# A hybrid attention layer on one core: transposes moved from TensorE to VectorE and DRAM, copies of sample rows in DRAM, state sums on VectorE

## The chip, the core and the metric

The kernel runs on one core of a Trainium2 chip. The metric is the device time of one execution in microseconds (us). A core has five engines that run their own instruction streams: PE (TensorE, matmuls and transposes), ACT (ScalarE), DVE (VectorE), POOL (GpSimd) and SP, which only issues DMAs here. POOL and ACT can issue DMAs too. Data lies in DRAM, in SBUF (128 partitions) and, for matmul outputs, in PSUM.

## What is computed

One inference step of a decoder layer with two mixers, for a prompt of 512 new tokens and for 8 running sequences with one new token each (the *samples*). Model width is 1024; all is float32. Cut to what the change touches:

```python
h = x @ w_in                                   # 1024 -> 3600 columns
qa, ka, va, za, ga, qb, kb, vb, gb = split(h)
# mixer A: gated linear attention, 4 heads, dk 64, dv 128, chunks of 64 tokens
S_t = diag(a_t) S_{t-1} + k_t^T v_t ;  o_t = q_t S_t     # samples: one step from state_gla
o_a = o_a * rsqrt(mean(o_a^2) + eps) * gla_norm_g
# mixer B: 8 heads of 64; keys at distances 0,d,2d,..,window for
# (window, d) = (128,1), (512,4), (2048,16), with a relative-position bias
o_b = merge of three softmaxes by their denominators    # samples: 1024 cached keys + the new one
mix = concat(o_a * silu(ga), o_b * silu(gb))
y   = mix @ w_out
x_new = layer_norm(sqrt(2) * x + y) * ln_g + ln_b
```

Outputs are x_new of prompt and samples, the final states of both, and the key and value rows to keep.

## The kernel before

Each product of a float32 matrix is made as three reduced-precision matmuls (high x high, high x low, low x high), so weights and activations are split into pairs named hi_ and lo_, mh and ml. The columns of w_in are worked off in pieces (qa, qb, kb, and so on); mixer B's prompt attention and mixer A's chunks run between them; and the output projection with w_out comes last: for tokens 0-255 (tiles y0, y1) the projection is first made with the tokens in the free dimension (ps_yf) and turned, for tokens 256-511 (y2, y3) with the tokens in the partitions (ps_y). The layer norm of a token tile runs on DVE and ACT as its last piece arrives. The sample rows travel as 8 further columns beside the prompt's.

**What sets the order.** The functions are generators that yield one operation at a time; a planner takes them as tasks and issues, engine by engine, the operation that its table TIMES has due first. TIMES holds one line per task, a start and the steps to each following operation, so it fixes the order on every engine. `At(mark)` holds a task until another one has set a mark; `Need(tag, ...)` holds it until a buffer of a kind is free (kinds: "g" for gate-sized tiles, "sv" for cached values, "r" for raw weights, and others). Every operation is recorded in the helper `issue`, so the profile gives line 672 for all of them, and groups are told apart by their tile names. QUEUE says which engine issues three kinds of turning DMAs: outputs y on POOL, values v on SP, keys k on POOL.

**Turning through DRAM.** `store_blocks` (line 1036) writes a tile, in which DVE has transposed each 32x32 block by itself, to a scratch array in DRAM, and `load_turned` (line 1040) reads the blocks back in exchanged places, which completes the transpose. Keys, values and the outputs of tokens 0-255 take this way: yw (blocks transposed) goes to ysc by a store, then yx comes from ysc by a load, both on POOL's queue, and DVE adds yx to y.

**mix_a(u, j)** (line 1926) finishes mixer A for 128 tokens: u is the half of the prompt, j the tile in it. oa holds o_a with tokens in partitions. Four PE transposes put it into a PSUM bank (ps_oat); three DVE operations multiply it by the norm's weight gn and the gate ga, and `split` makes the pair mha, mla for the output projection.

**The samples in mixer B.** `sample_queries` (line 1697) writes the 8 queries to DRAM (qsd) and reads each one back to all 128 partitions (qbc); POOL multiplies the cached keys (past) by it, DVE sums to logits. `sample_softmax` writes the probabilities to DRAM (psd_s), `sample_values` (line 1773) reads them back to the partitions of each cached-value tile (pb, 16 loads for 8 samples), and POOL multiplies (vv).

**sample_state** (line 1838) makes the samples' new states, four sequences at a time: s is the old state, v the new values read to all partitions. ACT multiplies s by the decay a_s (8 pieces of 128x128), SP writes it to the output; ACT multiplies v by the key ka_s (8 pieces), and POOL adds it to the output in DRAM by an accumulating DMA:

```python
for x, scale in ((s4, a_s), (v4, ka_s)):
    for bb in range(4):
        for m in range(2):
            yield S.mul(x[:, bb, m, :], x[:, bb, m, :], scale[:, m, i * 4 + bb:i * 4 + bb + 1])
    x = x.rearrange("p b m v -> p (b m) v")
    yield D.dma_start(to, x) if scale is a_s else G.dma_start(to, x, accum_op=ALU.add)
```

`last_norm` and `early_mean` close tile y3: early_mean takes the mean and variance of three quarters of the row ahead of time (tiles tail, mv), last_norm adds the last quarter behind the last matmul.

## Time and profile before

| | us |
|---|---|
| runs | 273.28, 274.27, 274.56 (median 274.27) |
| the profiled execution: time | 273.52 |
| the profiled execution: span | 271.7 |
| DMA traffic | 57.82 MB, mean 213 GB/s |
| last matmul ends (start 263.66, 0.28 long) | 263.94 |

The span is counted from the first to the last instruction in the trace; the execution's own time is 1.8 us longer. The page's second part cuts the span into 40 slices and gives each engine's busy share in tenths:

```profile
PE   8999999999999999999999999999999999999980
DVE  3844979999999877397999789687787586226994
POOL 3000000000183954550073451441916021611200
DMA  7995798244999798958999964979589995798132
```

A row of a timeline reads: start, duration, engine, line, operation, output tile <- input tiles with their shape, a count if neighbours are run together, and in brackets the idle time of the engine ahead of it and what ended it. The rows of a group read: busy time in all and mean ns of one, then idle time ahead of them and its releasers. Rows of stretches give, behind the bounds, the length and then the busy time of PE, PEld (weight loads), DVE, ACT and POOL, the granted clock, the DMA engines' share, and GB/s.

### The profile page before, as it was taken

How to read it: one execution, taken by the hardware profiler on the slowest of the kernel's cores; microseconds unless marked ns; L12 is line 12 of the kernel's file. 1: busy time of each engine (PE TensorE's matmuls, PEld its weight loads, DVE VectorE, ACT ScalarE, POOL GpSimd, SP SyncE). 2: the span in 40 equal slices, each digit the busy share in tenths (PEclk: the TensorE clock that was granted, in tenths of full speed). 3: DMA queues.
4: the chain of work that ended last, by engine and by line, in shares of the span. 5: the costliest groups of instructions: out<-in, count | busy, mean ns of one | idle time of the engine just before them, and what ended most of it. 6: DMA issues, size and time to landing. Idle time of an engine off the chain costs nothing. (4 is left out here: it accounts for less than half of the span.)

```text
span 271.7 us, 7366 instructions
## 1 busy us (share of the span) xinstructions
PE 262.8 (97%) x2851; PEld 247.2 (91%) x2851; DVE 209.3 (77%) x525; ACT 155.2 (57%) x462; POOL 77.4 (28%) x94
## 2 busy tenths in 40 slices
PE   8999999999999999999999999999999999999980
PEld 5999999999999999989989999989999999988880
DVE  3844979999999877397999789687787586226994
ACT  4735765565557763345956566536779855612720
POOL 3000000000183954550073451441916021611200
PEclk9999999999999999999999999999999999999995
DMA  7995798244999798958999964979589995798132
GB/s 207 354 251 127 188 280 212 74 120 131 280 309 202 221 317 157 303 148 253 271 232 328 292 177 143 270 176 281 167 214 245 286 230 89 159 322 179 77 154 82
DMA packets 70551, 57.82 MB, mean 213 GB/s; under 512 B 18157, under 2 KB 62355, under 8 KB 70517
## 3 DMA queue, kind: packets, MB, share of 16 engines
q1 hardware_dynamic: 67237, 53.36, 71.4%
q0 software_dynamic: 2848, 3.67, 7.1%
q8 instruction: 22, 0.36, 0.6%
q10 hardware_dynamic: 432, 0.33, 0.4%
q14 instruction: 12, 0.10, 0.1%
HBM read 48.31 MB, written 9.83 MB: 214 GB/s over the span
## 5 line engine op out<-in xcount | busy, mean ns | idle before, releaser
L672 POOL TENSOR_TENSOR past<-past,qbc 128x256 f32<-128x256 f32 x32 | 26.9, 871 | 82.5 <-DMA qbc<-qsd 81.0
L672 POOL TENSOR_TENSOR vv<-vv,pb 128x256 f32<-128x256 f32 x32 | 28.8, 930 | 43.6 <-DMA pb<-psd_s 40.8
L672 ACT ACTIVATE pr<-pr,ms 128x128 f32<-128x128 f32 (+3 forms) x48 | 22.8, 490 | 8.5 <-DVE ms L672 8.4
L672 ACT COPY pt<-ps_pt 128x256 f32<-128x256 f32 (+1 forms) x25 | 8.2, 347 | 9.5 <-PE ps_pt L672 9.4
L672 ACT ACTIVATE d<-d 128x512 f32<-128x512 f32 x11 | 6.9, 644 | 10.6 <-DVE d L672 10.6
L672 PE MATMUL ps_ka<-xx,hi_ka 128*128 128x264 f32 (+1 forms) x64 | 12.8, 295 | 0.0
L672 DVE CUSTOM_DVE_ANT_0 pr<-ps_s,strip 128x128 f32<-128x128 f32 (+3 forms) x32 | 11.7, 405 | 0.9 <-PE ps_s L672 0.9
L672 DVE TENSOR_REDUCE lt<-past 128x8 f32<-128x512 f32 x16 | 10.5, 671 | 0.7 <-POOL past L672 0.7
L672 PEld LDWEIGHTS ps_ka<-xx,hi_ka 128*128 128x128 f32 x64 | 10.3, 200 | 0.6 <-ACT hi_ka L672 0.6
L672 PE MATMUL ps_pt<-cf,pr 128*128 128x128 f32 x56 | 10.6, 276 | 0.3 <-DVE va L672 0.3
L672 DVE TENSOR_REDUCE o_pv<-vv 128x4 f32<-128x1024 f32 x8 | 9.7, 1208 | 0.0
L672 DVE SCALAR_TENSOR_TENSOR y<-y,yx 128x256 f32<-128x256 f32 x6 | 2.4, 420 | 8.8 <-DMA yx<-ysc 8.8
L672 PE MATMUL ps_ka<-xx,lo_ka 128*128 128x264 f32 (+1 forms) x32 | 9.0, 291 | 0.0
L672 DVE STREAM_TRANSPOSE yw<-feat_y 128x256 f32<-128x256 f32 x6 | 3.9, 642 | 5.6 <-ACT feat_y L672 5.6
L672 ACT CAST mhb<-gb 128x256 fp32r<-128x256 f32 x8 | 3.2, 406 | 8.2 <-DVE gb L672 7.6
L672 DVE TENSOR_SCALAR pr<-pr,ms 128x320 f32<-128x320 f32 (+3 forms) x16 | 7.7, 489 | 0.2
L672 PEld LDWEIGHTS ps_pt<-cf,pr 128*128 128x128 f32 x56 | 6.7, 140 | 1.0 <-DVE va L672 0.5
L672 ACT ACTIVATE qh<-ps_qb 128x128 fp32r<-128x128 f32 x16 | 5.2, 433 | 3.5 <-PE ps_qb L672 3.4
L672 ACT COPY feat_y<-ps_yf 128x256 f32<-128x256 f32 x8 | 3.0, 372 | 7.3 <-PE ps_yf L672 7.1
L672 DVE TENSOR_TENSOR gb<-gb,obT 128x256 f32<-128x256 f32 x8 | 6.1, 767 | 1.3 <-ACT gb L672 1.3
L672 PE MATMUL ps_pv<-pt,v 128*64 128x128 f32 (+1 forms) x80 | 6.9, 318 | 0.0
L672 DVE SCALAR_TENSOR_TENSOR ql<-ps_qb,qh 128x128 fp32r<-128x128 f32 x16 | 5.6, 397 | 1.6 <-ACT qk L672 1.5
(567 smaller groups left out, 1072.3 us busy)
## 6 DMA issues: line engine op xcount, KB each, us to landing
past<-in_ck_dram SPq DMA_DIRECT2D x8, 512.0 KB
vv<-in_cv_dram SPq DMA_DIRECT2D x8, 512.0 KB
pb<-psd_s SPq DMA_DIRECT2D x16, 256.0 KB
s<-in_state_dram SPq DMA_DIRECT2D x4, 512.0 KB
qbc<-qsd SPq DMA_DIRECT2D x8, 256.0 KB
y<-in_xp_dram SPq DMA_DIRECT2D x4, 512.0 KB
x_raw<-in_xT_dram SPq DMA_DIRECT2D x6, 260.0 KB
out_dram<-y SPq DMA_DIRECT2D x3, 512.0 KB
```

What stands on the lines that cost most here:

```text
L672: getattr(eng.eng, op.fn)(*op.args, **op.kw)
```

## The change

Three parts, and a new TIMES table.

1. **mix_a for tokens 0-255** no longer transposes on PE. DVE transposes the 32x32 blocks of oa into a "g" buffer ow, SP stores it to a new scratch array osc and reads it back turned, and the three multiplications read ow in place of PSUM. Tokens 256-511 keep their PE transposes.
2. **Sixteen copies.** qsd and psd_s hold each row 16 times, and a read takes each copy for 8 partitions. The order of heads and samples changes so that one read of pb covers the whole tile: 8 loads of 512 KB with rows of 4 KB in place of 16 loads of 256 KB with rows of 1 KB. Constants and the bias table follow the new order.
3. **sample_state** adds on DVE: ACT multiplies s as before, DVE computes s <- v * ka_s + s in 8 pieces, and one SP DMA writes the sum. ACT's pieces on v and the accumulating DMA go.

```diff
+COPIES = 16
-QUEUE = dict(y="G", v="D", k="G")
+QUEUE = dict(y="G", v="D", k="G", o="D")
...
-    qsd = dram.tile([NB, 512], F32, name="qsd")
-    psd_s = dram.tile([64, 256], F32, name="psd_s")
+    qsd = dram.tile([COPIES, 4 * NB + 4, P], F32, name="qsd")
+    psd_s = dram.tile([COPIES, 32 + 4, 256], F32, name="psd_s")
+    def reads(x, first, n, width):
+        return bass.AP(tensor=x.tensor, offset=x.offset + first, ap=[[x.shape[1] * x.shape[2], COPIES], [0, n // COPIES], [1, width]])
+    osc = {(u, j): scratch(f"osc{u}{j}", HA) for u in (0,) for j in range(2)}
...
     def sample_queries():
-        yield D.dma_start(by_tile(qsd), q_rows)
+        yield D.dma_start(qsd[:, :4 * NB].rearrange("r q d -> q r d"), q_rows[:, None, :].to_broadcast([32, COPIES, P]))
...
-            yield D.dma_start(qbc, qsd[bi:bi + 1, :].to_broadcast([P, 512]))
+            yield D.dma_start(qbc, reads(qsd, bi * 512, P, 512))
...
-        yield D.dma_start(psd_s, p_s[:, :256])
+        for v in range(2):
+            yield D.dma_start(psd_s[v * COPIES // 2:(v + 1) * COPIES // 2, :32].rearrange("r q k -> q r k"),
+                              p_s[v * 32:v * 32 + 32, None, :256].to_broadcast([32, COPIES // 2, 256]))
...
             pb = yield Need("sv", f"pb{bi}", [P, 4, 256])
-            row = psd_s[bi * 8:bi * 8 + 8, :]
-            for h2 in range(2):
-                yield D.dma_start(pb[h2 * 64:h2 * 64 + 64],
-                                  bass.AP(tensor=row.tensor, offset=row.offset + h2 * 256, ap=[[0, 64], [512, 4], [1, 256]]))
+            yield D.dma_start(pb.rearrange("p m k -> p (m k)"), reads(psd_s, bi * 1024, P, 1024))
...
     def sample_state():
-            for x, scale in ((s4, a_s), (v4, ka_s)):
-                for bb in range(4):
-                    for m in range(2):
-                        yield S.mul(x[:, bb, m, :], x[:, bb, m, :], scale[:, m, i * 4 + bb:i * 4 + bb + 1])
-                x = x.rearrange("p b m v -> p (b m) v")
-                yield D.dma_start(to, x) if scale is a_s else G.dma_start(to, x, accum_op=ALU.add)
-            free(v4, s4)
+            each = [(bb, m, i * 4 + bb) for bb in range(4) for m in range(2)]
+            for bb, m, n in each:
+                yield S.mul(s4[:, bb, m, :], s4[:, bb, m, :], a_s[:, m, n:n + 1])
+            for bb, m, n in each:
+                yield V.scalar_tensor_tensor(s4[:, bb, m, :], v4[:, bb, m, :], ka_s[:, m, n:n + 1], s4[:, bb, m, :], op0=ALU.mult, op1=ALU.add)
+            free(v4)
+            yield D.dma_start(to, s4.rearrange("p b m v -> p (b m) v"))
+            free(s4)
...
     def mix_a(u, j):
         yield At(f"oa_done{2 * u + j}")
+        oa = B[f"oa{u}"]
+        by_dram = not u
+        if by_dram:
+            ow = yield Need("g", f"ow{u}{j}", [P, HA, P])
+            yield blocks(ow, oa[:, j, :])
+            free(oa)
+            yield store_blocks(queue["o"], osc[u, j], ow)
+            yield load_turned(queue["o"], ow.rearrange("p h (a j) -> p (h a) j", j=32), osc[u, j])
         yield At(f"mla{u}")
         yield At(f"ga{u}_done", 4)
...
-        ps = yield bank("t", "ps_oat")
-        for hd in range(HA):
-            yield T.transpose(ps[:, hd * P:hd * P + P], oa[:, j, hd * P:hd * P + P], ident)
+        if not by_dram:
+            ps = yield bank("t", "ps_oat")
+            for hd in range(HA):
+                yield T.transpose(ps[:, hd * P:hd * P + P], oa[:, j, hd * P:hd * P + P], ident)
+            free(oa)
+            ow = ps.rearrange("p (h t) -> p h t", t=P)
```

New lines of TIMES for the tasks of the first part (before: 215978 and 216564, eight steps each):

```
mix_a|0|0 193600 1000 4400 17600 1358 489 884 1142
mix_a|0|1 198799 1 5835 12465 962 388 1446 585
```

**On SP, around the w_out loads.** The rows of SP's queue around the last four w_out loads, before (raw_wo are the pieces of w_out, v<-vad the samples' values, s the samples' states, y<-in_xp the residual rows; in brackets what a row waits for):

```order
L672 DMA v_3435<-vad 64x8x128 [waits DVE_49]
L672 DMA raw_wo__3444<-in_w_out_dram 128x2x512 [waits DMAHW6_49,Activation_49]
L672 DMA v_3435<-vad 64x8x128 [waits DMAHW7_49]
L672 DMA raw_wo__3477<-in_w_out_dram 128x2x512 [waits DMAHW0_49,DMAHW1_49,DVE_49,Activation_49]
L672 DMA raw_wo__3548<-in_w_out_dram 128x2x512 [waits DMAHW2_49,DVE_49,Activation_49]
L672 DMA out_dram<-s_3264 128x8x128 [waits Activation_49]
L672 DMA raw_wo__3595<-in_w_out_dram 128x2x512 [waits DMAHW6_49,DMAHW3_49,DVE_49]
L672 DMA y_3642<-in_xp_dram 128x1024 [waits DMAHW4_49,PE_49]
```

and now:

```order
L677 DMA osc_103<-ow_3296 128x4x128 [waits DMAHW6_49,DVE_49]
L677 DMA v_3333<-vad 64x8x128 [waits DVE_49]
L677 DMA v_3333<-vad 64x8x128 [waits DMAHW0_49]
L677 DMA ow_3296<-osc_103 128x16x32 [waits DMAHW6_49,DMAHW1_49,PE_49]
L677 DMA osc_104<-ow_3442 128x4x128 [waits DMAHW2_49,DVE_49]
L677 DMA raw_wo__3460<-in_w_out_dram 128x2x512 [waits DMAHW3_49,Activation_49]
L677 DMA raw_wo__3492<-in_w_out_dram 128x2x512 [waits DMAHW4_49,DVE_49,Activation_49]
L677 DMA ow_3442<-osc_104 128x16x32 [waits DMAHW5_49,DMAHW2_49,PE_49]
L677 DMA raw_wo__3558<-in_w_out_dram 128x2x512 [waits DVE_49,Activation_49]
L677 DMA raw_wo__3597<-in_w_out_dram 128x2x512 [waits DMAHW7_49,DMAHW3_49,DVE_49]
L677 DMA y_3644<-in_xp_dram 128x1024 [waits DMAHW0_49,PE_49]
```

The two stores and two loads of ow stand among the last four w_out loads, and the write of the first states (out_dram<-s) has left this place; it stands behind the loads of w_s and avg now, and that of the second states behind y, gamma and beta.

**On DVE, ahead of mixer A's gate.** Where lo_wo__3605, the products of the third last w_out piece, is made, the rows before:

```order
L672 TENSOR_TENSOR lo_wo__3605<-raw_wo__3477,hi_wo__3604 128x512
L672 SCALAR_TENSOR_TENSOR ga_3237<-ps_oat,gn,ga_3237 128x2x128 x2
L672 SCALAR_TENSOR_TENSOR ga_3237<-ps_oat,gn,ga_3237 128x2x64 x4
```

and now (lo_wo__3607 is the same piece):

```order
L677 SCALAR_TENSOR_TENSOR s_3275<-v_3333,ka_s,s_3275 128x128 x2
L677 TENSOR_TENSOR lo_wo__3607<-raw_wo__3492,hi_wo__3606 128x512
L677 SCALAR_TENSOR_TENSOR s_3275<-v_3333,ka_s,s_3275 128x128 x3
L677 SCALAR_TENSOR_TENSOR ga_3241<-ow_3296,gn,ga_3241 128x2x128
L677 SCALAR_TENSOR_TENSOR ga_3241<-ow_3442,gn,ga_3241 128x2x128
L677 SCALAR_TENSOR_TENSOR ga_3241<-ow_3296,gn,ga_3241 128x2x64
L677 SCALAR_TENSOR_TENSOR ga_3241<-ow_3442,gn,ga_3241 128x2x64
```

The first eight state sums stand directly ahead of the multiplications by the gate, and these read ow.

**On POOL, the end of its queue.** Before (ysc and yx are store and load of the turned outputs):

```order
L672 DMA out_dram<-v_3435 128x8x128
L672 DMA ysc_95<-yw_3803 128x4x128
L672 DMA ysc_96<-yw_3837 128x4x128
L672 DMA yx_3891<-ysc_95 128x16x32
L672 DMA yx_3928<-ysc_96 128x16x32
L672 DMA ysc_97<-yw_3875 128x4x128
L672 DMA out_dram<-v_3729 128x8x128
L672 DMA yx_4016<-ysc_97 128x16x32
```

and now:

```order
L677 DMA ysc_96<-yw_3797 128x4x128
L677 DMA ysc_97<-yw_3831 128x4x128
L677 DMA yx_3884<-ysc_96 128x16x32
L677 DMA ysc_98<-yw_3869 128x4x128
L677 DMA yx_3916<-ysc_97 128x16x32
L677 DMA yx_3983<-ysc_98 128x16x32
```

Both accumulating DMAs are gone, and the third store stands ahead of the second load.

More of the change, by code (lines that the diff above doesn't have):

```diff
@@ L109, in __init__ @@
             run = 4 * min(run_of(x) for x in aps)
-            rate = 130 if run <= 128 else 175 if x.ap[0][1] <= 64 else 340 if run >= 4096 else 230
-            self.xfer = max(4 * total(x) / rate, 200)
+            rows = x.ap[0][1] * (x.ap[1][1] if x.ap[1][0] == 0 else 1)
+            y = aps[aps[0].tensor.space != bass.MemoryType.DRAM]
+            copies = math.prod(c for step, c in y.ap[1:] if step == 0)
+            rate = 130 if run <= 128 else 175 if rows <= 64 else 340 if run >= 4096 else 230
+            copied = total(x) // copies
+            self.xfer = max(4 * copied / rate, 200)
             self.late = 600 * (rate == 175)
@@ L247 @@
+evac|ps_ka00|0 23728 1
 evac|ps_ka10|0 24419 175
@@ L297 @@
+evac_f|ps_vb0_f1|1 83824a 2706 -191 588 8171
+sample_logit|3|past3|qbc3 89592 154 1 1177 2468 1220
+evac|ps_vb0_2|2 90137a
 scores|0|1 89774 946
-evac|ps_vb0_2|2 90137a
+sample_logit|4|past4|qbc4 96447 700 1354 1 2215 995
+softmax|1|2|ps_s12|pr12 91602 1396 981 150a 26274 273 1407 108 581a
 softmax|0|2|ps_s02|pr02 91359 1327 1444 871a 23920 823 1 1 1a
-softmax|1|2|ps_s12|pr12 91602 714 1663 150a 26274 273 1407 218 471a
+softmax|0|3|ps_s03|pr03 92687 554 949 804a 23928 827 242 109 299a
+softmax|1|3|ps_s13|pr13 92692 548 2460 1352 23352 1 1569 218 145
@@ L376 @@
-softmax|7|3|ps_s73|pr73 167352 2344 1267 122a 8 2024 1707 1 5
-evac_f|ps_va1_f1|1 169131 66 1808 78 6
+scores|3|1 164789 1
+softmax|6|2|ps_s62|pr62 165736 1619 1519 345 831 521 2064 798 217a
+softmax|6|3|ps_s63|pr63 166837 1902 793 190 1063 299 2131 109 557a
+softmax|7|2|ps_s72|pr72 165733 1100 525 249a 2540 249 38 138 306a
+softmax|7|3|ps_s73|pr73 167352 2344 699 690a 8 2024 1707 1 371a
+sample_value|5|vv5|pb5 184673 7 2 1 5285
+evac_f|ps_va1_f0|0 165732 1 411 3 5a
+evac_f|ps_va1_f1|1 167605a 1a 3399 78 425a
@@ L744, in trunk @@
     ssq, rmss = cst("ssq", [P, TT * HA]), cst("rmss", [P, TT * HA])
-    q_s, k_s = cst("q_s", [P, 4, NB]), cst("k_s", [P, 4, NB])
+    q_w, k_w = cst("q_s", [P, NB, 4]), cst("k_s", [P, NB, 4])
+    q_s, k_s = (x.rearrange("p b m -> p m b") for x in (q_w, k_w))
     q_rows = cst("q_rows", [32, P])
@@ L964, in fills @@
         raw = B["rb_raw"]
-        yield S.copy(rb[:64], raw)
-        yield V.tensor_tensor(rb[32:64], raw[32:], rb[32:64].bitcast(F32), op=ALU.subtract)
+        to, by_v = rb.rearrange("p v b m -> p b v m"), raw.rearrange("p b (m v) -> p b v m", v=2)
+        yield S.copy(to[:64], by_v)
+        yield V.tensor_tensor(to[32:64], by_v[32:], rb.bitcast(F32).rearrange("p v b m -> p b v m")[32:64], op=ALU.subtract)
+        yield S.copy(rbt.rearrange("p (v m) -> p v m", v=2), rb[:, :, 0])
         free(raw)
@@ L1062, in sample_rows @@
         ps = yield bank("t", "ps_rows")
-        yield T.transpose(ps[:32, :P], x.rearrange("p m b -> p (m b)"), ident)
+        yield T.transpose(ps[:32, :P], x, ident)
         yield copy(rows, ps[:32, :P])
@@ L1233, in bias_table @@
             pt = yield bank("t", "ps_tab")
-            yield T.matmul(pt[:HB, :c.stop - c.start], rb[:, 0, :], ct[:, c], start=True, stop=True)
+            yield T.matmul(pt[:HB, :c.stop - c.start], rbt, ct[:, c], start=True, stop=True)
             yield copy(tsb[:, to], pt[:HB, :c.stop - c.start])
@@ L1512, in sample_v @@
             yield V.memset(rows, 0.0)
-        yield from sample_rows(x, rows[:32])
+        yield from sample_rows(x.rearrange("p m b -> p (m b)"), rows[:32])
         yield D.dma_start(out, rows[:32])
@@ L1698, in sample_queries @@
         yield At("qb", 8)
-        yield from sample_rows(q_s, q_rows)
-        yield D.dma_start(by_tile(qsd), q_rows)
+        yield from sample_rows(q_w.rearrange("p b m -> p (b m)"), q_rows)
+        yield D.dma_start(qsd[:, :4 * NB].rearrange("r q d -> q r d"), q_rows[:, None, :].to_broadcast([32, COPIES, P]))
         for bi in range(NB):
@@ L1714, in sample_logit @@
         for k in range(2):
-            yield V.tensor_reduce(lt[:, k, bi * 8:bi * 8 + 8], past[:, k].rearrange("p (h d) -> p h d", d=64), axis=AX.X, op=ALU.add)
+            yield V.tensor_reduce(lt[:, k].rearrange("p (v b m) -> p b m v", v=2, b=NB)[:, bi],
+                                  past[:, k].rearrange("p (m v d) -> p m v d", v=2, d=64), axis=AX.X, op=ALU.add)
         free(past)
@@ L1725, in sample_softmax @@
         k_rows = yield Need("t1", "k_rows", [32, P])
-        yield from sample_rows(k_s, k_rows)
-        yield D.dma_start(by_tile(kw_s), k_rows)
+        yield from sample_rows(k_w.rearrange("p b m -> p (b m)"), k_rows)
+        yield D.dma_start(kw_s.rearrange("b (m d) -> (b m) d", d=P), k_rows)
         prod = yield Need("t1", "prod", [32, P])
```

233 lines of the change are left out of this document (111 added, 122 removed).

## The prediction

> **What bounds the kernel now.** I read the page's busy table first, then the table of stretches, then the waits of PE, then the chain that ended last.
>
> ```profile
> PE 262.8 (97%) x2851; PEld 247.2 (91%) x2851; DVE 209.3 (77%) x525; ACT 155.2 (57%) x462; POOL 77.4 (28%) x94
> ...
> 4.00:264.00 260.00, 259.61 (x2845) 245.97 (x2843) 204.02 (x504) 152.64 (x458) 75.09 (x86) 1.00 0.82 218
> 264.00:271.70 7.70, 0.00 (x0) 0.00 (x0) 4.17 (x13) 0.83 (x3) 0.00 (x0) 0.64 0.21 72
> ...
> PE warm_ps L672 <- PEq L2354: 0.8, 1, 0.8
> PE ps_pt L672 <- DVE va L672: 0.3, 1, 0.3
> ```
>
> From 4 to 264 us PE is busy 259.61 of 260 us at a granted clock of 1.00, and it waits 1.1 us in the whole program. Up to 264 us, only fewer or shorter matmuls, or a new wait of PE, can move the time. Waits of POOL and ACT up to there cost nothing now. Behind PE's last matmul lie 7.7 us in which VectorE closes the last rows. The chain of waits says what came last there:
>
> ```profile
> 253.94 3.00 DVE y L672 x3
> ...
> 267.95 0.40 DVE y L672
> ```
>
> From 253.94 us to the end the chain lies on VectorE alone, ten us before PE is done. So the end has two near bounds, PE's last matmul and VectorE's own queue, and I need to know by how much VectorE is late:
>
> ```profile
> 260.80 0.28 PE L672 MATMUL ps_y<-hi_wo__3484,mla 128*128 128x258 f32 x1
> 263.66 0.28 PE L672 MATMUL ps_y<-hi_wo__3484,mla 128*128 128x256 f32 x1
> ...
> 250.48 0.76 DVE L672 SCALAR_TENSOR_TENSOR y<-y,yx 128x256 f32<-128x256 f32 x2 [2.13 <-DMA yx<-ysc]
> ...
> 262.28 0.41 DVE L672 SCALAR_TENSOR_TENSOR y<-y,ps_y 128x256 f32<-128x256 f32 x1
> 266.80 1.54 DVE L672 SCALAR_TENSOR_TENSOR y<-y,tail,beta 128x256 f32<-128x256 f32 x3
> ...
> 263.97 0.47 ACT L672 ACTIVATE sq_y<-ps_y,tail 128x256 f32<-128x256 f32 x1 [4.60 <-PE ps_y L672]
> ```
>
> The second-last output group (128x258) ends at 261.08 us, and VectorE reads it at 262.28: it is 1.2 us late. Its last idle time is the 2.13 us before 250.48, in which it waits for the load of yx; after that its queue is full until 266. If that load came early enough, the close would hang on PE alone: ACT's square starts 0.03 us behind the last matmul either way, and VectorE's last three writes could stand up to 1.2 us nearer to it.
>
> **The change part by part.**
>
> *Transposes of tokens 0-255.* Eight PE transposes go (two tiles of four); those of tokens 256-511 stay.
>
> ```profile
> 215.31 1.04 PE L672 MATMUL ps_oat<-cf,oa 128*128 128x128 f32 x8
> 216.10 0.37 PE L672 MATMUL ps_yf<-mhb,hi_wo__3268 128*128 128x264 f32 x1
> ```
>
> The eight start at 215.31 and the next matmul at 216.10, so PE gains 0.79 us. All that follows on PE moves up by this, if nothing new holds it. In their place stand two VectorE stream transposes of 128x512, two stores and two loads of 256 KB on SP's queue. The multiplications by the gate stay and read SBUF in place of PSUM; I cost that swap at nothing, since it changes an operand only (the same instruction on PSUM: 1.90 us for six).
>
> ```profile
> L672 DVE STREAM_TRANSPOSE kx<-kd 128x512 f32<-128x512 f32 x2 | 2.1, 1100 | 0.0
> ...
> 216.38 1.90 DVE L672 SCALAR_TENSOR_TENSOR ga<-ps_oat,gn,ga 128x256 f32<-128x256 f32 x6
> 218.98 1.28 DVE L672 TENSOR_TENSOR mla<-ga,mha 128x512 fp32r<-128x512 f32 x2
> ...
> 224.35 0.28 PE L672 MATMUL ps_yf<-mha,hi_wo__3438 128*128 128x264 f32 x1
> ...
> 205.00:216.00 11.00, 11.00 (x95) 11.00 (x94) 6.30 (x15) 9.42 (x37) 3.71 (x5) 1.00 0.93 242
> ...
> 200.44 0.15 DVE L672 TENSOR_TENSOR lo_wo__3329<-wsum,hi_wo__3328 128x4 fp32r<-128x4 f32 x1
> ```
>
> Two transposes of 1.10 us cost VectorE 2.2 us. They hide: it is busy 6.30 of 11 us in 205-216. The round trip is the risk. The new order puts the second transpose directly ahead of the row that ran at 200.44, so it would end near 201.6, and its store can go about 203, behind a load of v. PE needs mla at 224.35 now, 223.56 with the gain; behind the load stand half of the six multiplications (0.95) and both halves of mla (1.28), 2.2 us. So store and load together may take 223.6 - 2.2 - 203 = **18.4 us** before PE waits. The nearest rows are the outputs' own round trip, of the same 256 KB and the same 32x32 blocks:
>
> ```profile
> L672 POOL DMA_DIRECT2D yx<-ysc x3: 1153/1163/1171, 232.5 to 245.5; - x3
> ...
> DMA to landing us min/median/max: 5.0/8.6/9.4
> ...
> L672 POOL DMA_DIRECT2D ysc<-yw x3: 756/767/798, 228.8 to 236.2; - x3
> ...
> DMA to landing us min/median/max: 2.8/2.8/8.6
> ```
>
> Shortest 2.8 + 5.0 = 7.8 us, median 11.4, longest 8.6 + 9.4 = 18.0. All fit, the longest by 0.4 us. I take the median and cost the round trip at nothing. SP's queue holds four w_out loads between and behind these DMAs; the last two of them now wait for the second load to be issued:
>
> ```profile
> 211.40 0.37 SPq L672 DMA_DIRECT2D raw_wo__3595<-in_w_out_dram  x1
> ...
> 224.98 0.68 DVE L672 TENSOR_TENSOR lo_wo__3742<-raw_wo__3595,hi_wo__3741 128x512 fp32r<-128x512 f32 x1
> ```
>
> The load of ow goes when the store has landed, 203 + 2.8 to 203 + 8.6, that is 206 to 212; the last w_out load goes at 211.40 now and its last product is made at 224.98, thirteen us later. I cost this at nothing too.
>
> *New states on VectorE.* Sixteen ACT multiplications (v by ka) go, sixteen 128x128 VectorE operations come, and the two 512 KB accumulating DMAs of POOL's queue go.
>
> ```profile
> L672 DVE SCALAR_TENSOR_TENSOR st<-st,el,ps_kv 128x128 f32<-128x128 f32 x14 | 3.8, 342 | 0.7 <-PE ps_kv L672 0.7
> ...
> L672 ACT ACTIVATE v<-v,ka_s 128x128 f32<-128x128 f32 x16 | 5.3, 412 | 0.0
> ...
> 241.93 0.76 DVE L672 SCALAR_TENSOR_TENSOR y<-y,yx 128x256 f32<-128x256 f32 x2 [6.04 <-DMA yx<-ysc]
> ...
> 236.20 0.77 POOL L672 DMA_DIRECT2D ysc<-yw  x1
> 237.29 1.59 POOL L672 DMA_DIRECT2D out_dram<-v  x1 [0.32 <-issue]
> 245.50 1.17 POOL L672 DMA_DIRECT2D yx<-ysc  x1 [6.62 <-DVE y L672]
> ...
> 232.64 0.40 SPq L672 DMA_DIRECT2D out_dram<-s  x1
> ```
>
> VectorE pays 14 in 3.8 us, 0.27 each, so 2.2 us for each eight, at most 8 x 0.342 = 2.7. The first eight stand ahead of the multiplications by the gate and take from the idle 4.7 us of 205-216 what the transposes left (2.5). The second eight stand at about 236-241, where VectorE sits idle 6.04 us: nothing. ACT's 5.3 us are not on the path.
>
> What the missing accumulations give is at the third yx. The accumulation was issued at 237.29, directly behind the third ysc store, and the yx load behind them went only at 245.50, with VectorE's part done by 242.7. One of the three ysc stores landed after 8.6 us, the others after 2.8; that it is the third fits, 236.20 + 8.6 = 244.8, so I read the load as waiting for this store. With 512 KB less beside them and with the y loads placed earlier in SP's order (they wait behind the state write at 232.64 now), I expect the third yx one to three us earlier. From below it is nothing, if the other bytes of the stretch are what held the store; from above it is the whole 2.13 us of idle time plus PE's 0.79. VectorE can use at most its lateness of 1.2 us on top of PE's gain. I take 0.8 of it, since the first two yx gain as well.
>
> *Sixteen copies of queries and probabilities.* The bytes that the readers move stay; each copy now serves 8 partitions, and the rows of pb become 4 KB.
>
> ```profile
> L672 POOL TENSOR_TENSOR past<-past,qbc 128x256 f32<-128x256 f32 x32 | 26.9, 871 | 82.5 <-DMA qbc<-qsd 81.0
> L672 POOL TENSOR_TENSOR vv<-vv,pb 128x256 f32<-128x256 f32 x32 | 28.8, 930 | 43.6 <-DMA pb<-psd_s 40.8
> ```
>
> POOL waits 81.0 and 40.8 us for these loads. PE's table of waits has no row that leads back to them, so any gain ends in POOL's idle time: I take nothing. From both sides: PE's other 0.3 us could go, or a load that comes late could cost it something like that.
>
> *Sum.* PE -0.8, VectorE's lateness -0.8, all else 0: -1.6 us. The profiled run took 273.52 us (span 271.7 and 1.8 around it), which gives 271.9. The three runs have their median at 274.27, 0.75 above the profiled one; -1.6 from there is **272.7 us**.
>
> **The Trainium skill on POOL's queue.** The same accumulating DMA is issued twice in the trace:
>
> ```profile
> 217.92 1.64 POOL L672 DMA_DIRECT2D out_dram<-v  x1 [9.04 <-ACT v L672]
> ```
>
> It took 1.64 us here with VectorE busy on two-input operations beside it (216.38 to 220.26) and 1.59 us at 237.29 with VectorE idle. The Trainium skill, SBUF — State Buffer, section "SBUF: two separate sides", says that VectorE and GpSimd hold a common port pair by an exclusive lock, and that descriptors of GpSimd's DMAs cannot be written while VectorE has it. The two durations do not show this. By the rule, the second eight new operations, which stand among GpSimd's ysc and yx issues, would hold these up; what that would cost by this case's rows is rival E.
>
> **The rivals.**
>
> A, the forecast: PE gains 0.8 and the third yx frees VectorE by 0.8. 272.7.
>
> ```profile
> 246.93 0.28 DVE L672 TENSOR_REDUCE sums_s<-w_s 64x1 f32<-64x128 f32 x1
> ...
> 247.62 0.23 PE L672 MATMUL ps_ms<-sums_s,avg 66*66 66x1 f32 x2
> ```
>
> B, PE gains but the close does not follow. The load of yx stays where it is, because the DMA engines carry nearly the same bytes there, or PE meets a new short wait for the sums of the sample rows (VectorE's reduction ends 247.21 and PE reads it at 247.62 now, so 0.4 us are left against a PE that comes 0.8 earlier). For it: VectorE's queue, not PE, sets the last ten us. Then 0 to -0.8: 273.5 to 274.3.
>
> The two accumulating DMAs of out_dram, by the view of their tile:
>
> ```profile
> DMA to landing us min/median/max: 9.9/11.1/12.3
> ```
>
> C, slower: PE waits for mla at the first matmul on mha, since the round trip through DRAM takes over 18.4 us. It decides from there, one us of time for each us beyond. For it: the DMA engines are at 0.93 in 205-216, and the 512 KB writes of POOL's queue landed after 9.9 to 12.3 us. With 11 us for each leg the sum is 22, PE waits 3.6 us, and -0.8 + 3.6 gives +2.8: about 277. Against it: the legs have half those bytes.
>
> D, the close follows in full: -0.8 - 1.2 = -2.0, and PE's 0.3 us may go too: 272.0 to 272.3.
>
> E, the eight VectorE operations hold the yx issues: up to 8 x 0.342 = 2.7 us on loads that had one to three to gain; the close stays late and PE's gain is lost: 274.3.
>
> **How the numbers follow.** A measurement of this kernel can tell about 0.5% from no change, 1.4 us here. A 0.36, D 0.14, B 0.34, C 0.11, E 0.05. A lies at -0.6%, just beyond the bound, so some of its spread counts as the same: faster 0.46 (D and most of A), same 0.40, slower 0.14 (C, and what E and B could add). The range goes from D with a little more from the DMAs, 271.2, to B and E with the scatter of the runs (273.28 to 274.56), 275.0; C beyond that is left out.
>
> **What would show it.** Right: 8 matmuls fewer, PE's last one 0.8 us earlier, no row of PE waiting for mla, the third yx issued before 243 us, and VectorE's idle time before its last additions of yx gone. B: the last matmul earlier and the span not, with a wait for yx as before. C: a PE wait at mha or mla near 224. E: yx issues of clearly over 1.17 us. Wrong in another way: a PE wait anywhere in 185-215, where the w_out loads and the state write now stand in another order on SP's queue.

## The result and the profile after

| | before | after |
|---|---|---|
| runs, us | 273.94 (273.20 to 274.56, 6 runs) | 271.75 (271.44 to 272.57, 6 runs) |
| ratio of the runs, 95% interval | | 0.9924 [0.9899, 0.9948] |
| the profiled execution: time; span | 273.52; 271.7 | 271.75; 270.0 |
| the last matmul starts | 263.66 | 263.06 |
| VectorE's last three writes start | 266.80 | 265.30 |

The kernel became faster by 2.2 us (1.4 to 2.8). The forecast was 272.7, 1.6 us faster. Medians here and below leave out three slow executions: 426.4 us (run a_copies) and 366.8 us (the kernel before) at granted clocks of 0.56 and 0.66, and 275.97 us (run b_state). First the busy table of the changed kernel, its stretch from 242 to 250 us, and PE's waits:

```profile
PE 261.9 (97%) x2843; PEld 245.7 (91%) x2843; DVE 218.6 (81%) x540; ACT 152.3 (56%) x450; POOL 72.2 (27%) x92
...
242.00:250.00 8.00, 8.00 (x40) 6.50 (x39) 4.84 (x17) 1.69 (x3) 1.05 (x3) 1.00 0.15 38
...
PE warm_ps L677 <- PEq L2381: 0.8, 1, 0.8
PE ps_pt L677 <- DVE va L677: 0.6, 1, 0.6
```

PE has eight matmuls fewer. VectorE is busy 9 us longer, and the only wait of PE for it, the one for va, is 0.6 in place of 0.3. From 242 to 250 us the DMA engines are nearly idle (0.15). Before, the stretch from 244 to 248 alone showed this:

```profile
244.00:248.00 4.00, 4.00 (x20) 3.23 (x19) 3.89 (x13) 0.00 (x0) 1.17 (x1) 1.00 1.27 265
```

Now the timeline rows of the changed kernel that answer to those of the prediction: the first output matmul behind the place of the eight transposes, the end of the second-last output group and of the last, and VectorE's and POOL's rows of the close:

```profile
215.44 0.28 PE L677 MATMUL ps_yf<-mhb,hi_wo__3263 128*128 128x264 f32 x1
...
260.20 0.28 PE L677 MATMUL ps_y<-hi_wo__3498,mla 128*128 128x258 f32 x1
...
263.06 0.28 PE L677 MATMUL ps_y<-hi_wo__3498,mla 128*128 128x256 f32 x1
...
248.81 0.15 DVE L677 COPY sums_s<-ps_vs 64x1 f32<-64x1 f32 x1 [1.12 <-PE ps_vs L677]
248.88 0.74 DVE L677 SCALAR_TENSOR_TENSOR y<-y,yx 128x256 f32<-128x256 f32 x2
...
260.79 0.41 DVE L677 SCALAR_TENSOR_TENSOR y<-y,ps_y 128x256 f32<-128x256 f32 x1
...
265.30 1.54 DVE L677 SCALAR_TENSOR_TENSOR y<-y,tail,beta 128x256 f32<-128x256 f32 x3
...
235.38 0.76 POOL L677 DMA_DIRECT2D ysc<-yw  x1 [2.27 <-DVE yw L677]
236.13 1.16 POOL L677 DMA_DIRECT2D yx<-ysc  x1
...
241.03 1.16 POOL L677 DMA_DIRECT2D yx<-ysc  x1 [3.74 <-DMA ysc<-yw]
```

The third yx is issued at 241.03 (before 245.50), VectorE adds it without a DMA wait (the 1.12 us ahead of the last additions are a wait for PE's ps_vs), and it reads the second-last group 0.31 us behind its end (260.48) where it was 1.20 us late.

**Where the 1.5 us at VectorE's last writes came from.** I set the two traces side by side at the same matmuls. The first matmul of the bias table, which stands in the same place of PE's queue in both, started at

```profile
28.93 0.39 PE L672 MATMUL ps_tab<-ct,rb 66*8 66x512 f32 x1
...
28.42 0.40 PE L677 MATMUL ps_tab<-ct,rbt 66*8 66x512 f32 x1
```

before and after. Over the ten profiles below whose programs follow the changed kernel up to there, this start lies between 28.09 and 28.99 (mean 28.68), over the four that follow the kernel before between 28.48 and 28.93 (mean 28.77): the half microsecond of this pair is scatter of the start, not the change. In this pair it arises between 5 and 7 us, where PE starts 14 matmuls before and 22 after, though the rows of both stretches give a granted clock of 1.00. Behind it PE's lead runs 0.51 at 28 us, 0.36 at 134, -0.14 at 153, 0.66 at 215.4 (216.10 - 215.44), 0.60 at the end. So the change itself lost 0.15 up to 134, lost 0.5 around 143, gained 0.80 with the transposes, and lost 0.06 behind them. The close gained 266.80 - 263.66 - (265.30 - 263.06) = 0.90.

| step | profiled pair, us |
|---|---|
| scatter of the start | -0.5 |
| PE, 28 to 215 us, without the transposes | +0.65 |
| PE, transposes | -0.8 |
| PE behind them | +0.06 |
| VectorE's close | -0.9 |

### The profile page after: what moved, and what is told of

Its sections match the earlier page's. It is cut to its first block, busy times and chain, and to the rows that moved or that the text cites. A ratio compares the mean times of both kernels' runs of the same rounds, so it can differ in the third digit from the quotient of the medians.

```text
span 270.0 us, 7350 instructions
## 1 busy us (share of the span) xinstructions
PE 261.9 (97%) x2843; PEld 245.7 (91%) x2843; DVE 218.6 (81%) x540; ACT 152.3 (56%) x450; POOL 72.2 (27%) x92
## 4 chain that ended last, share of the span: by engine, by line
PE 88%; DVE 9%; issue 1%; ACT 0%; DVEq 0%
PE ps_gb L677 9%; PE ps_qb L677 9%; PE ps_yf L677 9%; PE ps_kb L677 9%; PE ps_ga L677 9%; PE ps_qa L677 5%; PE ps_ka L677 4%; PE ps_vb_f L677 4%; PE ps_vb L677 4%; PE ps_va L677 4%; DVE y L677 4%; PE ps_y L677 3%; PE ps_s L677 3%; PE ps_va_f L677 3%; PE ps_pt L677 2%; PE ps_pv L677 2%
## 5 line engine op out<-in xcount | busy, mean ns | idle before, releaser
L677 POOL TENSOR_TENSOR vv<-vv,pb 128x256 f32<-128x256 f32 x32 | 25.6, 832 | 44.4 <-DMA pb<-psd_s 30.0
L677 ACT ACTIVATE pr<-pr,ms 128x288 f32<-128x288 f32 (+3 forms) x52 | 24.8, 494 | 11.4 <-DVE ms L677 11.3
L677 POOL DMA_DIRECT2D ysc<-yw x3 | 2.4, 786 | 24.9 <-DVE yw L677 24.9
L677 DVE RECIPROCAL ms<-ms 128x1 f32<-128x1 f32 x32 | 4.6, 155 | 2.9 <-ACT pr L677 2.9
L677 DVE TENSOR_TENSOR xx<-x_raw,xx 128x520 fp32r<-128x520 f32 (+2 forms) x10 | 5.8, 589 | 1.3 <-ACT xx L677 1.2
L677 PE MATMUL ps_s<-kp,qh 64*128 64x256 f32 (+1 forms) x64 | 6.8, 302 | 0.0
L677 DVE TENSOR_TENSOR d<-b 128x1024 f32<-128x1024 f32 (+1 forms) x6 | 6.7, 1124 | 0.0
```

The lines of the kernel that those rows point to most:

```text
L677: getattr(eng.eng, op.fn)(*op.args, **op.kw)
```

## The experiments

Times are medians with the number of runs. The kernel before was run beside them and had medians of 273.78 to 273.86; the changed kernel was not, so differences from it are taken to its 271.75.

**1. The transposes back on PE (pe_turn), in the changed kernel.**

```diff
-        by_dram = not u
+        by_dram = False
```

with the two table lines of before for these tasks.

> The changed kernel with the eight PE transposes of tokens 0-255 put back (no ow, no osc, two VectorE transposes and four SP DMAs fewer). Theory 1 (the change gains through PE's eight transposes and through VectorE's end separately): PE's last matmul 0.8 us later than in the changed kernel (263.06 there), VectorE's last additions of yx still without a DMA wait, time about +0.8 (272.5). Rival (VectorE's queue alone sets the end, PE's gain is spare): the same time within 0.3, 271.7.

Measured 273.3 (12 runs). PE's last matmul starts at 264.31; its start was 0.49 late, so 1.25 - 0.49 = 0.76 is the transposes:

```profile
216.00 1.04 PE L677 MATMUL ps_oat<-cf,oa 128*128 128x128 f32 x8
216.79 0.37 PE L677 MATMUL ps_yf<-mhb,hi_wo__3263 128*128 128x264 f32 x1
```

Theory 1 holds in sign and, in the trace, in size; the median moved by twice as much (1.55), of which the trace shows half.

**2. The states as before (accum), in the changed kernel.**

```diff
-            for bb, m, n in each:
-                yield V.scalar_tensor_tensor(s4[:, bb, m, :], v4[:, bb, m, :], ka_s[:, m, n:n + 1], s4[:, bb, m, :], op0=ALU.mult, op1=ALU.add)
...
-            yield D.dma_start(to, s4.rearrange("p b m v -> p (b m) v"))
...
+            for x, scale in ((s4, a_s), (v4, ka_s)):
...
+                        yield S.mul(x[:, bb, m, :], x[:, bb, m, :], scale[:, m, i * 4 + bb:i * 4 + bb + 1])
...
+                yield D.dma_start(to, x) if scale is a_s else G.dma_start(to, x, accum_op=ALU.add)
```

> The changed kernel with the states made as before: ACT multiplies v, SP writes s early, POOL adds v to the output by two accumulating DMAs; the table line of this task is that of before, PE's order stays. Theory 1 (the accumulation and the early state write held the third yx): the third yx load issued at 244-245 us instead of 241, VectorE waits for yx again by 1-2 us ahead of its last additions of it, PE's last matmul unmoved near 263.1, time +0.8 to +1.3 (272.6 to 273.0). Rival (the gain at the end comes from the new order of other work): VectorE's last writes within 0.3 of 265.30, time +-0.3.

Measured 273.7 (12 runs), 1.95 slower, more than theory 1 said. The third yx load came back to near where it was (244.75), as theory 1 said, but the loss runs another way: VectorE's last additions of yx do not wait for it, and PE, which theory 1 left unmoved, got two waits that I had not expected. POOL, VectorE and PE of this run:

```profile
244.75 1.17 POOL L677 DMA_DIRECT2D yx<-ysc  x1 [4.36 <-DMA ysc<-yw]
...
246.34 0.76 DVE L677 SCALAR_TENSOR_TENSOR y<-y,yx 128x256 f32<-128x256 f32 x2 [3.73 <-DMA yx<-ysc]
249.19 0.26 DVE L677 TENSOR_REDUCE sums_s<-w_s 64x1 f32<-64x128 f32 x1
...
249.55 0.25 PE L677 MATMUL ps_ms<-sums_s,avg 66*66 66x1 f32 x2 [0.94 <-PE ps_y L677]
...
216.62 0.39 PE L677 MATMUL ps_yf<-mhb,hi_wo__3263 128*128 128x264 f32 x1 [0.66 <-ACT mhb L677]
```

The second yx is late to VectorE (246.34), the sample rows' reduction stands behind it in VectorE's queue, and PE's matmul starts 0.1 us after the reduction ends, 0.94 us idle. The profile names another matmul of PE as releaser; by the times it was the reduction. This is the place with 0.4 us of room that the prediction named in rival B. The other wait is the samples' mhb at 216.6: ACT waits 2.8 us for a w_out piece that SP issued at 205.24 (203.47 in the changed kernel), and three multiplications of v (0.97 us) stand ahead of the cast again. PE's last matmul starts at 265.66, 2.60 later, and VectorE's last three writes at 267.91, 2.25 behind it. That is the distance of the changed kernel (2.24; 3.14 before): in this order the late yx costs through PE's waits and not through VectorE's close.

**3. The states alone, in the kernel before (b_state):** the edit of 2 turned round, with that task's new table line.

> The kernel before with the states made on VectorE and written once by SP, with that task's line of the order table from the changed kernel; nothing else changed. Theory 1 (the accumulating DMAs hold the third yx and VectorE's end): the third yx load near 241 us instead of 245.5, no DMA wait of VectorE ahead of its last additions of yx, PE's last matmul unmoved, time -0.8 to -1.2. Rival (the parts only help together with the new order): PE or VectorE get a wait for the eight new operations ahead of the gate, time 0 to +0.5.

Measured 272.77 (8 runs), ratio 0.9951 [0.9921, 0.9982]: 1.0 us faster by the medians, 1.3 by the ratio. The wait ahead of the last additions fell from 2.13 to 0.94 us, and the last writes stand at 266.25 (before 266.80) though PE's last matmul was 0.6 us later in this execution: they follow it by 2.01 us in place of 3.14. The third yx was issued at 244.48, not at 241. VectorE was done with the first yx at 243.27; what ended last was the third ysc store, issued at 237.00 and landed after 6.9 us (8.6 before). VectorE's additions of the first and of the third yx:

```profile
242.51 0.76 DVE L672 SCALAR_TENSOR_TENSOR y<-y,yx 128x256 f32<-128x256 f32 x2 [4.87 <-DMA yx<-ysc]
249.88 0.76 DVE L672 SCALAR_TENSOR_TENSOR y<-y,yx 128x256 f32<-128x256 f32 x2 [0.94 <-DMA yx<-ysc]
```

**4. Is it the accumulation, or the new place of the y loads? (y_late, in the changed kernel.)**

```diff
-residual|2 237548
-residual|3 237549
+residual|2 242500
+residual|3 242501
```

> The changed kernel with the two loads of y for tokens 256-511 issued by SP behind the second write of the states, about 16 us later than now; states still on VectorE, no accumulating DMA. Theory 1 (the accumulating DMA itself held the third yx): the third yx is issued near 241 and lands as now, time within 0.4, apart from a wait of VectorE for the y rows themselves. Rival (what freed the third yx is that the y loads fell into the idle stretch at 223 to 232): yx and ysc land later (7 us and more in place of 4.5), VectorE waits for yx, time +0.8 or more.

Measured 272.11 (6 runs), 0.36 from the changed kernel. SP issues the y loads at 239.28 in place of 222.78, and the third yx goes even earlier:

```profile
238.75 1.16 POOL L677 DMA_DIRECT2D yx<-ysc  x1 [1.17 <-DMA ysc<-yw]
```

So the new place of the y loads is not needed: a later one frees yx even more. But this run does not tell the accumulation from the y loads, because neither is beside the third ysc store any more. Its landing, by the view of its tile, is what the third yx load waits for in all five traces:

| | y loads go | second accumulating DMA goes | third store goes | lands after, us | third yx goes |
|---|---|---|---|---|---|
| before | 233.15 | 237.29 | 236.20 | 8.6 | 245.50 |
| accum | 233.92 | 238.78 | 236.87 | 7.2 | 244.75 |
| b_state | 224.09 | none | 237.00 | 6.9 | 244.48 |
| changed | 222.78 | none | 235.38 | 5.1 | 241.03 |
| y_late | 239.28 | none | 235.66 | 2.6 | 238.75 |

The third yx goes 0.5 to 0.7 us after the landing each time. So the prediction read this wait rightly, and what is transferred beside the store holds it. Runs 2 and 3 put the accumulation, the early write of s and the place of the y loads in and out together; which of them held the store before stays open.

**5. The transposes alone, in the kernel before (b_turn).** `mix_a`, `osc`, QUEUE and the two table lines from the changed kernel.

> The kernel before with only the transposes of tokens 0-255 moved to VectorE and DRAM, with the two lines of the order table for it. Theory 1 (PE's gain does not reach the end while VectorE waits for the third yx): PE's last matmul 0.7 to 0.8 us earlier, the third yx load at most 0.8 us earlier, time 0 to -0.8. Rival (VectorE has room in every case): -0.8 or more.

Measured 278.56 (6 runs), ratio 1.0155 [1.0120, 1.0190]: 4.8 us slower by the medians, 4.2 by the ratio. Neither theory had this. SP's queue, POOL, VectorE and PE of this run:

```profile
202.60 1.47 SPq L672 DMA_DIRECT2D osc<-ow  x1
204.16 1.25 SPq L672 DMA_DIRECT2D pb<-psd_s  x2
...
210.13 1.43 POOL L672 TENSOR_TENSOR vv<-vv,pb 128x256 f32<-128x256 f32 x2 [13.27 <-DMA pb<-psd_s]
...
215.42 1.21 DVE L672 TENSOR_REDUCE o_pv<-vv 128x4 f32<-128x1024 f32 x1
...
219.34 0.59 PE L672 MATMUL ps_yf<-mhb,hi_wo__3270 128*128 128x264 f32 x1 [4.14 <-ACT mhb L672]
```

Read it downwards: the last load of the samples' probabilities stands on SP behind the second store of ow, and goes at 204.16 where it went at 196.24 in the kernel before. POOL's products, VectorE's sum, the gate and the cast mhb follow one another, and PE waits 4.1 us at its first output matmul. PE goes on as soon as the first of the two casts of mhb has ended. In the kernel before, this one ended 1.36 us ahead of PE's first output matmul (216.10), and 0.57 us ahead of the transposes that stood before it (215.31):

```profile
214.50 0.24 ACT L672 CAST mhb<-gb_s 128x16 fp32r<-128x16 f32 x1
```

In the changed kernel the last pb goes at 188.39, eight us earlier, as one DMA.

The wait is not the whole loss. PE's first output matmul is 3.2 us later than in the kernel before, its last one 6.1 us. Behind the wait PE ran at half its rate; the same stretch in the kernel before and in this run:

```profile
219.34:225.20 5.86, 5.86 (x52) 5.86 (x51) 4.97 (x13) 2.32 (x6) 0.22 (x1) 1.00 1.30 191
...
219.34:225.20 5.86, 5.86 (x26) 5.86 (x27) 4.78 (x13) 4.61 (x13) 1.64 (x1) 0.50 0.96 279
```

The granted clock is 0.50 for these 5.9 us, and 26 matmuls stand where there were 52. PE falls back by a further 2.7 us here, of the 6.1 in all.

**6. The same with the last pb ahead of ow on SP (b_turn_pb).**

```diff
-sample_values ... 605 6653 9578 1
+sample_values ... 605 6653 4600 1
```

> b_turn (the kernel before with only the transposes moved; 4.6 us slower than before, PE waited 4.1 us at 215 us for the samples' mhb) with one step of the order table earlier: SP issues the last two loads of pb ahead of the first store of ow. Theory (the sample values' chain, last pb - POOL's products - sum - gate - mhb, has about a us of room ahead of PE, and the round trip of ow on SP's queue took it): PE's wait for mhb is gone or under 0.5 us, PE's last matmul 0.5 to 0.8 us earlier than in the kernel before, time 273.0 to 274.0. Rival (the DMAs of the round trip themselves, or VectorE's two transposes, make mhb late): a wait of 2 us or more stays, time 276 or more.

Measured 276.8 (6 runs); PE's wait fell from 4.1 to 2.2 us, not to 0.5. These are the rival's numbers, but the rows point to another cause than its own: pb was one part, and the rest is the next load on the same queue. ACT waits for a w_out piece, which SP issued at 206.11 (201.22 in the kernel before). ACT's work on it stands ahead of the samples' cast in ACT's queue, and VectorE's product of it ahead of the samples' sum:

```profile
206.11 0.60 SPq L672 DMA_DIRECT2D raw_wo__3453<-in_w_out_dram  x1
...
212.45 0.62 ACT L672 CAST hi_wo__3553<-raw_wo__3453 128x512 fp32r<-128x512 f32 x1 [3.45 <-DMA raw_wo__3453<-in_w_out_dram]
217.37 0.23 ACT L672 CAST mhb<-gb_s 128x16 fp32r<-128x16 f32 x1
```

By these rows both waits come from what the round trip stands in front of on SP; its own data was in time, since PE has no wait for mha or mla in either run. Behind this wait, too, the granted clock is low: 0.53 from 218.6 to 222.2.

**7. The copies. One source for everything (one_source), one source for the queries (qbc_one), both parts undone (a_copies).**

```diff
-ap=[[x.shape[1] * x.shape[2], COPIES], [0, n // COPIES], [1, width]]
+ap=[[0, COPIES], [0, n // COPIES], [1, width]]
```

> The changed kernel, but all partitions read their queries and probabilities from the first of the sixteen copies; the copies are still written and no order changes. Theory 1 (the copies only fill POOL's idle time): qbc and pb land later than 4.6 and 7.5 us, POOL waits longer, time within 0.3. Rival (faster pb loads put POOL's products beside VectorE's and made PE's wait at 143 us longer, 0.27 to 0.63): that wait shrinks toward 0.3 and the time falls by 0.3. Other rival (the copies bring time): +0.5 or more, by a new wait of PE.

In this run the upper 64 partitions get the probabilities of the other four heads, since the copies of psd_s are kept by halves; the samples' outputs are other numbers, the work is the same. Measured 273.81 (12 runs, 271.65 to 274.38): 2.1 us slower, on the side of the last rival. PE has three waits where it had one:

```profile
PE ps_pt L677 <- DVE va L677: 0.4, 1, 0.4
PE ps_vb L677 <- ACT v L677: 0.4, 1, 0.4
PE ps_pt L677 <- DVE pt L677: 0.3, 1, 0.3
```

> The changed kernel with the sample queries read from one copy by all 128 partitions; the probabilities keep their copies. After one_source (2.1 us slower, with new PE waits at 120, 147 and 151 us): Theory (the slow reads of qbc hold the cached keys' buffers and with them SP's queue, so that a load behind them comes late to ACT and PE waits at 120 us): qbc lands after 5.5 us or more, the wait at 120 us is there (0.4 to 0.7), those at 147 to 166 are not, time +0.6 to +1.2. Rival (only the probabilities matter): no wait at 120 us, time +-0.3.

Measured 271.98 (8 runs), no wait at 120 us: the queries' copies bring nothing here that can be seen, the rival holds. If the two losses add, the probabilities' single source costs the other 1.8 us by the medians. That is not shown: of the 2.1 us of PE's last matmul in one_source's profile 0.6 are the start, 0.7 lie between 143 and 166 us, and 0.6 at 120 us, ahead of the first load of pb (132.03). Nor do the two runs read the queries alike: qbc landed after 5.7 us in the median in one_source and after 4.5 in qbc_one, whose access pattern is another one (4.6 in the changed kernel). In one_source PE has no wait for mhb, so it is not the sixteen copies that make room for the transposes; the single load of pb and the new order are left, and no run separates these.

The third of them has the edits of 1 and 2 together:

> The changed kernel with both the transposes put back on PE and the states made as before: the copies and the new order of the rest are what is left of the change. Theory (the copies gain nothing by themselves, they give the sample values' chain room that the transposes then use): the last pb is issued near 188 us, the samples' mhb is ready earlier than in the kernel before, PE has no new wait, time 273.5 to 274.3, as before. Rival (copies and order carry a gain of their own): 273.0 or less.

Measured 274.46 (11 runs), ratio 1.0021 [1.0003, 1.0038]. The copies and the new order gain nothing alone; the wait for the sample rows' sums (1.0 us at ps_ms, as in run 2) makes them a little slower than before. This closes the account by the medians: taking back both parts costs 2.7 us (1.55 and 1.95 one by one, so they overlap), and what is left is 0.6 slower than the kernel before; 2.7 less 0.6 is the change's gain.

**8. Can the changed kernel be bettered? (va_first, both, best.)** Three moves of the order table:

```diff
-mix_b|1|0 140511 425 1473
+mix_b|1|0 141500 425 1473
```

> The changed kernel with one line of the order table moved: the copy va<-ps_turn stands ahead of the product gb<-gb,obT on VectorE. Theory (PE waits at 143 us for this copy alone, behind a product of 1.15 us that runs beside POOL): PE's wait there (0.63) goes to 0 to 0.1, PE's last matmul is 0.6 to 0.8 us earlier, the time falls by 0.3 to 0.8, less where VectorE's lateness of 0.3 us at the end returns. Rival (PE waits for something else there, or VectorE sets the end): the wait stays, or it goes and the time stays within 0.2.

Measured 271.51 (6 runs), the fastest kernel here, by 0.24, which these runs can't tell from none and which lies between the theory's 0.3 and the rival's 0.2. The 0.63 at 143 us is gone and 0.3 came back at 145.7 (ps_pt, waiting for a copy of VectorE); less the start, PE's last matmul gained 0.14 + 0.34 = 0.48 us.

The run both moves the last additions of yx forward as well (`out_evac|0|2|yx2 249000 10`, `out_evac|1|2|yx2 249005 10`):

> The changed kernel with va<-ps_turn ahead of gb<-gb,obT (as va_first) and with VectorE's last additions of yx ahead of its copy of ps_vs. Theory (VectorE is still 0.3 us late at the second last output group and waits 1.1 us for ps_vs ahead of the additions, with yx landed 2 us before): VectorE reads the second last group without lateness, its last writes follow PE's last matmul 0.3 us closer, time -0.3 to -0.5 against the changed kernel (271.2 to 271.5). Rival (the close hangs on PE already): the same as va_first, 271.5.

Measured 272.72 (12 runs), slower than va_first. The additions ran at 247.63, but the norm's steps behind them went along and pulled ACT's rstd ahead of the samples' square; PE waited for that:

```profile
249.04 0.29 ACT L677 ACTIVATE rstd<-mv,ln_eps 128x1 f32<-128x1 f32 x1 [7.41 <-DVE mv L677]
249.25 0.29 ACT L677 ACTIVATE sq_s<-w_s 64x128 f32<-64x128 f32 x1
...
249.68 0.28 PE L677 MATMUL ps_vs<-sums_s,avg 66*66 66x1 f32 x2 [0.97 <-ACT sq_s L677]
```

The run best holds those steps back (`norm|0 249700 ...`) and puts both products gb behind the copies (`mix_b|1|0 149000`, `mix_b|1|1 149400`):

> The changed kernel with two moves in the order table: the two products gb<-gb,obT of one half go behind the copies that PE waits for at 143 to 150 us, and VectorE's last additions of yx go ahead of its copy of ps_vs, while the steps behind them stay behind it (in the kernel both they overtook the samples' square on ACT and PE waited 1.0 us for it). Theory: PE's wait at 143 us is gone without a new one at 146, PE's last matmul 0.5 us earlier, VectorE on time at the end; time 270.8 to 271.4. Rival (PE finds another wait, as in va_first): 271.5 to 272.

Measured 272.46 (6 runs): the wait for the square is gone, and PE found another, 0.8 us at ps_pt for a copy of ACT. The rival holds; none of the three is a clear gain.

## Why the prediction was right, and where not

- **PE -0.8 from the transposes:** right: 0.80 in the pair, 0.76 in run 1.
- **VectorE's lateness -0.8 of at most 1.2:** right in size, 0.89 (1.20 to 0.31), and in its step: the third store landed after 5.1 us in place of 8.6 and the third yx went 4.5 us earlier. Run 3 shows the state part as the cause in the old order, where VectorE's last writes came 1.13 us nearer to PE's last matmul. In the new order, taking it back costs as much and more, but through waits of PE (run 2). Whether the y loads help by going earlier, as the forecast also said, stays open: in run 4 they go later, and the store lands after 2.6 us.
- **The round trip at nothing, 18.4 us of room:** right in the changed kernel, where three of its four DMAs stand ahead of the last four w_out loads and one among them. The second store went at 203.01 as forecast, its load at 206.69, and PE did not wait at mha. But the step "I cost this at nothing too", for SP's loads between and behind the round trip, was right only in the new order. I looked for a late ow (rival C) and should have looked at what stands behind it on SP: in the old order the same move costs 4.8 us (run 5), through a chain of the samples whose 1.36 us of room I did not read, though its rows are in the trace of before, and through the low clock behind the wait.
- **The copies at nothing:** right where this part stands alone (a_copies gains nothing), wrong as a price of it within the change, and the result hid this. "PE's table of waits has no row that leads back to them" says that nothing is lost there now; it does not say how much room there is. The single load of pb and the new order moved the last pb from 196.24 to 188.39, ahead of the round trip, and PE has no wait for mhb. In the new order a single source for queries and probabilities costs 2.1 us (run 7), by which of them is open.
- **New operations on VectorE at nothing:** right for PE at the gate and for yx. Rival E is refuted: the third ysc was issued at 235.38 in 0.76 us, wholly beside five new operations on VectorE (235.01 to 236.37), and the second yx behind it in 1.16 us, both as long as before.
- **Not in the sum:** PE's longer wait at 143 us and small losses ahead of it, 0.65 us together. The forecast named the 0.3 us there as something that might go or come, and took nothing. By these terms the pair of traces gives -0.8 - 0.9 + 0.7 = -1.0 without the start's scatter, while the medians moved by 2.2 (at least 1.4 by the interval). The difference of 0.4 to 1.2 us I can't place in the traces: one execution of each kernel was traced, and run 1's median also moved by more than its trace. So two terms were right by their mechanism, and that their sum of -1.6 came as near to -2.2 as it did is in part luck.

The 143 us wait: PE's ps_pt waits for VectorE's copy va, which should come 0.51 earlier than before by the start and came 0.10 earlier. Two VectorE products of 128x512 (lo_va) stand ahead of it; both with the copy and POOL's rows, before:

```profile
140.13 0.68 DVE L672 TENSOR_TENSOR lo_va__2382<-raw_va__2057,hi_va__2381 128x512 fp32r<-128x512 f32 x1
...
141.07 0.68 DVE L672 TENSOR_TENSOR lo_va__2382<-raw_va__2057,hi_va__2381 128x512 fp32r<-128x512 f32 x1
...
143.31 0.41 DVE L672 COPY va<-ps_turn 128x256 f32<-128x256 f32 x1
...
136.65 3.41 POOL L672 TENSOR_TENSOR vv<-vv,pb 128x256 f32<-128x256 f32 x4 [17.49 <-DMA pb<-psd_s]
141.07 4.14 POOL L672 TENSOR_TENSOR vv<-vv,pb 128x256 f32<-128x256 f32 x4 [1.01 <-DMA pb<-psd_s]
```

and the second of them after:

```profile
140.79 1.22 DVE L677 TENSOR_TENSOR lo_va__2381<-raw_va__2061,hi_va__2380 128x512 fp32r<-128x512 f32 x1
...
143.21 0.42 DVE L677 COPY va<-ps_turn 128x256 f32<-128x256 f32 x1
...
136.58 7.79 POOL L677 TENSOR_TENSOR vv<-vv,pb 128x256 f32<-128x256 f32 x8 [19.59 <-DMA pb<-psd_s]
```

Before, POOL was idle from 140.06 to 141.07, waiting for pb, and the first piece fell into that gap; the second began at 141.07 together with POOL's next products, took 0.68 too, and POOL's four products took 0.73 longer than the four ahead of them. With the faster loads POOL multiplies eight pieces without a gap, and both pieces of VectorE (the first at 138.77) take 1.22, 1.08 more together. VectorE's order differs a little there too, so these 1.08 us are the likely cause of the lost 0.41, not a measured one. Run one_source points the same way: there POOL's products begin only at 140.30, the piece at 139.51 took 0.69 us, the one at 141.93 took 1.22 beside them, and PE's wait for va was 0.36. The Trainium skill, SBUF — State Buffer, section "SBUF: two separate sides", says that a VectorE operation with two SBUF inputs and a GpSimd operation that reads SBUF take one port pair in turn, the later one waiting. The rows agree: the later VectorE piece took 0.54 longer, and POOL's products took 0.73 longer where VectorE began with them. The forecast had taken rival E from the same section of the Trainium skill, but that section limits the two-input case to a GpSimd operation that reads SBUF; POOL only issued DMAs there, and its issues (0.76 and 1.16 us) show no delay.

## What to carry to other kernels

A new order that gains nothing by itself can still make the room that another part needs: read, for each stream of loads, the room between the end of its chain and the engine that reads it, because the next edit on the same queue spends that room. When a transfer is put into a queue, price what stands behind it there, not only its own round trip. A wait of PE can cost more than its length: read the granted clock behind it. And before a difference of half a microsecond between two traces is explained, compare them at a matmul ahead of the first edit.

## What had not been expected of the hardware

A VectorE product of two SBUF operands took 0.68 us at 128x512 where POOL was idle and 1.22 us beside POOL's products; in the extreme a 128x1024 product took 4.51 us (another of this size, begun at 135.68 while POOL was idle, took 1.22):

```profile
88.48 4.51 DVE L677 TENSOR_TENSOR lo_kb__1395<-raw_kb__956,hi_kb__1394 128x1024 fp32r<-128x1024 f32 x1
...
88.42 5.17 POOL L677 TENSOR_TENSOR past<-past,qbc 128x256 f32<-128x256 f32 x6
```

It began 0.06 us after a run of six POOL products and ended 0.6 us before the run did.

After PE had waited 4.1 us, its granted clock was 0.50 for 5.9 us (run 5), and after 2.2 us it was 0.53 for 3.6 us (run 6). After waits of 0.9 to 1.0 us (accum, both, a_copies) it stayed at 1.00. Ten profiles of programs that are alike up to 28 us reached that place with a scatter of 0.9 us.
